# Feed-forward entry of a hybrid decoder block on one core: turned tiles and late sums kept in raw weight places, and the first product of the third weight pair moved ahead of the first pair's middle

## The chip, the cores and the metric

The kernel runs on one core of one Trainium2 chip. The metric is device time in microseconds (us) of one execution. Engines are named as the profile names them: PE (TensorE, matmuls), PEld (its weight loads), DVE (VectorE), ACT (ScalarE), POOL (GpSimd), SP (SyncE, which issues most DMAs; SPq is its queue). Each engine works through its own instructions in order and waits on semaphores for the others.

## The reference, cut to what matters

One decoder block over 1024 tokens of 1024 channels in float32: a state-space branch and a forgetting-attention branch, merged and projected, then cross-attention into 256 memory tokens, then the feed-forward part that the change is about, then a last normalisation.

```python
h = h + (gate_a * out_a + gate_b * out_b) @ w_mix_out[l]          # "mix"
h = h + memory_cross_attention(...)                               # ends with  o @ w_mem_o
f_a, f_b = jnp.split(rms_norm(h, norm_ffn[l]) @ w_ffn_in[l], 2, axis=-1)   # 1024 x (2 x 2816)
h = h + (jax.nn.silu(f_a) * f_b) @ w_ffn_out[l]                   # 2816 x 1024
return rms_norm(h, norm_final)
```

## The kernel before, in words

**Precision.** Every operand of a large product is split into a rounded high part and the remaining low part (`B.split`: ACT casts the high part, DVE subtracts for the low part), and each product is three matmuls: high x high, high x low, low x high (`mm3`, and `prod` in the feed-forward part). A matmul here has 512 columns.

**The feed-forward up-projection.** The hidden width 2816 is 22 blocks of 128. Block j needs 128 columns of the first half of `w_ffn_in` and 128 of the second: a "weight pair" of two 512 KB loads (`raw`, `rawb`). The product of a pair with the activations is done as seven half-size products in place of eight (Strassen's scheme in Winograd's form). Its left operands are sums of weight quarters, its right operands are quarters of the normalised and transposed ("turned") activations and sums of them: A11, A12, A22, S1, S2, S3, S4. Each product is 12 matmuls. Per pair the code has three parts:

- `start(j)`: products 1 (A11) and 2 (A12), into banks `mm` and `sc`; ACT and DVE then make silu of their sum.
- `middle(j)`: products 6 (S2), 7 (S3) and 5 (S1).
- `end(j)`: products 3 (S4) and 4 (A22), and the gated result.

The weights come from `w_first(j)` (products 1 and 2), `w_sums(j)` (5, 6, 7: `whi`/`wlo` and `we`) and `w_last(j)` (3, 4: `wdh`/`wdl`). From pair 2 on they are split on chip from `raw` and `rawb`. For pairs 0 and 1 (`AHEAD_IN = 2`) that was done much earlier, among the mix products (`ahead(j)`), and kept in DRAM (`w_d`), so that here they are only loaded.

**The entry.** `norm_blocks(t)` takes tile t of 128 tokens: DVE scales it (`xs`, line 220), PE turns it (line 226, eight 128x128 transposes into a `misc` and a `pv` bank), and the quarters and sums are split. Tiles 0 to 3 give A11 and A12; tiles 4 to 7 give the rest, and each needs the turned tile t - 4 again. In the kernel before, tiles 0 to 3 go to DRAM (`x_d`, 8 writes of 256 KB) and are read back as `xa` (4 reads of 512 KB). S4 and A22 are needed last, so their sources go to DRAM as well (`r_d`, 8 writes) and are read back in `norm_rest` as `xr` (4 reads).

**Order.** The code is recorded and then ordered by a scheduler that works from dependencies, so instructions of neighbouring steps are interleaved on each engine. Places in on-chip memory come from pools: "raw" has four places for weights before their split, "tmp" four places of 128 x 1024, "t" sixteen and "big" sixteen. A new tile waits until the last reader of the place is done. All the loads of the entry are issued by SP, in order.

Of the kernel before, what the change touches and what calls it, by code (L numbers as in the profile page):

```python
# [9 lines left out]
F32 = mybir.dt.float32  # L10
F32R = mybir.dt.float32r
# [8 lines left out]
P = 128  # L20
D = 1024
# [45 lines left out]
def f32(ap):  # L67
    return ap.bitcast(F32)
# [26 lines left out]
def weave(main, side, lead=0):  # L95

    n, m, done = len(main) - lead, len(side), 0
    for i, f in enumerate(main):
        f()
        want = m if i + 1 == len(main) else max(0, (i + 1 - lead) * m // max(n, 1))  # L100
        while done < want:
            side[done]()
            done += 1


class Shared:
# [3 lines left out]
        self.pool = pool  # L110

    def tmp(self, name, dt=F32):
        return self.pool.tile([P, D], dt, tag="tmp", bufs=4, name=name)

    def half(self, name, dt=F32):
        return self.pool.tile([P, 512], dt, tag="half", bufs=5, name=name)
# [386 lines left out]
def stage_tail(B, big, s2, sh, x, glu, aT, gate_d, kv_d, w_fox_o, w_mix_out, g_mq, w_mem_q, w_mem_o, g_ffn,  # L503
# [7 lines left out]
    def slot(dt=F32, name="t"):  # L511
        return s2.tile([P, D], dt, tag="t", bufs=NS2, name=name)
# [79 lines left out]


    AHEAD_IN = 2
    w_d = B.dram.tile([AHEAD_IN, 7, P, D], F32, name="w_d")
    pre = {}

    def ahead(j):

        def keep(n, t_):  # L600
            A.dma_start(w_d[j, n], f32(t_))

        def pair(n):
            hl = tmp("wph", F32R), tmp("wpl", F32R)
            return hl, [[t_[:, o:o + 512] for t_ in hl] for o in (0, 512)]

        def fetch():
            pre[j] = [tmp("wpr") for _ in range(2)]
            for r_, c in zip(pre[j], (0, FH)):
                S.dma_start(r_.rearrange("p (k c) -> p k c", k=8),  # L610
                            w_ffn_in[:, c + j * P:c + (j + 1) * P].rearrange("(k p) c -> p k c", p=P))

        def plain():
            hl, _ = pair(0)
            B.split(*hl, pre[j][0])
            for i, t_ in enumerate(hl):
                keep(i, t_)

        def sums():
            ra, rb = pre[j]  # L620
            b22 = rb[:, 512:]
            hl, (w5, w6) = pair(2)
            V.tensor_add(ra[:, 512:], ra[:, 512:], b22)
            V.tensor_add(ra[:, :512], ra[:, :512], rb[:, :512])
            V.tensor_add(rb[:, :512], rb[:, :512], b22)
            B.split(*w5, ra[:, :512])
            V.tensor_add(ra[:, 512:], ra[:, 512:], ra[:, :512])
            V.tensor_add(ra[:, :512], ra[:, :512], b22)
            B.split(*w6, ra[:, :512])
            for i, t_ in enumerate(hl):  # L630
                keep(2 + i, t_)

        def seventh():
            e_ = tmp("wph", F32R)
            B.split(e_[:, :512], e_[:, 512:], pre[j][1][:, :512])
            keep(4, e_)

        def rest():
            ra, rb = pre.pop(j)
            hl, (w3, w4) = pair(5)  # L640
            B.split(*w3, rb[:, 512:])
            B.split(*w4, ra[:, 512:])
            for i, t_ in enumerate(hl):
                keep(5 + i, t_)

        return [fetch, plain, sums, seventh, rest]

    wm0 = mix_weights(0)
    wm1 = mix_weights(1)
    mixes = [lambda t=t: mix(t, 0, wm0) for t in range(NT)] + [lambda t=t: mix(t, 1, wm1) for t in range(4)]  # L650
    weave(mixes, [f for j in range(AHEAD_IN) for f in ahead(j)], 4)
    for t in range(4, NT):
        mix(t, 1, wm1)
        norm(t - 4, gq, u2)
# [60 lines left out]
    def mem_out(t):  # L715
        oh, ol = oT[t // 4]
        for c in range(2):
            cs = slice(512 * c, 512 * c + 512)
            ps = B.bank()
            for h in range(MH):  # L720
                o = (h % 2) * 512 + (t % 4) * P
                B.mm3(ps, oh[h // 2][:, o:o + P], ol[h // 2][:, o:o + P], wo[h][0][:, 0, cs], wo[h][1][:, 0, cs],
                      h == 0, h == MH - 1)
            V.tensor_add(H[t][:, cs], H[t][:, cs], ps)
# [23 lines left out]

    NF = FH // P
    h_d = B.dram.tile([NT, P, D], F32, name="h_d")  # L750
    x_d = B.dram.tile([4, P, D], F32, name="x_d")
    r_d = B.dram.tile([4, P, D], F32, name="r_d")
    comb = {}

    def blocks(name, mk):
        if name not in comb:
# [3 lines left out]
    def put(name, mk, i, src, neg=False):  # L760

        hi_, lo_ = blocks(name, mk)
        for kk in range(2):
            sv = src[:, kk * 256:(kk + 1) * 256].rearrange("p (k c) -> p k c", k=2)
            hi, lo = [a[kk][:, :, i * P:(i + 1) * P] for a in (hi_, lo_)]
            if neg:
                A.activation(hi, sv, AF.Copy, scale=-1.0)
                V.scalar_tensor_tensor(out=lo, in0=sv, scalar=-1.0, in1=f32(hi), op0=ALU.mult, op1=ALU.subtract)
            else:
                B.split(hi, lo, sv)  # L770

    def norm_blocks(t):
        i = t % 4
        xs = s2.tile([P, D], F32, tag="xs", bufs=1, name="xs")
        B.norm_scale(xs, H[t], B.rstd(H[t]), gf)
        S.dma_start(h_d[t], H[t])
        ps = [B.turn(xs, b, ("misc", "pv")[b]) for b in range(2)]
        if t < 4:
            for b in range(2):
                xf = sh.half("xf")  # L780
                A.copy(xf, ps[b])
                S.dma_start(x_d[i][:, 512 * b:512 * b + 512], xf)
                put(("A11", "A12")[b], slot, i, xf)
            return
        xa, sx, s3 = tmp("xa"), tmp("sx"), sh.half("s3")
        S.dma_start(xa, x_d[i])
        a11, a12, s1n, a22 = xa[:, :512], xa[:, 512:], sx[:, :512], sx[:, 512:]
        A.copy(a22, ps[1])
        V.tensor_sub(s3, a11, ps[0])
        V.tensor_sub(s1n, ps[0], a22)  # L790
        V.tensor_sub(a11, s1n, a11)
        V.scalar_tensor_tensor(out=a12, in0=a11, scalar=-1.0, in1=a12, op0=ALU.mult, op1=ALU.subtract)
        put("S2", slot, i, a11)
        put("S3", bslot, i, s3)
        put("S1", bslot, i, s1n, neg=True)
        S.dma_start(r_d[i][:, :512], a12)
        S.dma_start(r_d[i][:, 512:], a22)

    def norm_rest(i):
        y = tmp("xr")  # L800
        S.dma_start(y, r_d[i])
        put("S4", bslot, i, y[:, :512])
        put("A22", bslot, i, y[:, 512:])

    raws, wts, ev = {}, {}, {}

    def w_fetch(j):
        raws[j] = B.wpool.tile([P, RAW], F32, tag="raw", bufs=4, name="raw")[:, :D], tmp("rawb")
        for r_, c in zip(raws[j], (0, FH)):
            f = S.dma_start(r_.rearrange("p (k c) -> p k c", k=8),  # L810
                            w_ffn_in[:, c + j * P:c + (j + 1) * P].rearrange("(k p) c -> p k c", p=P))
        return f

    def wpair(j):
        if j < 0:
            return slot(F32R, "wh0"), slot(F32R, "wl0")
        return [B.wpool.tile([P, WSLOT], F32R, tag=t_, name=t_)[:, :D] for t_ in ("whi", "wlo")]

    def w_kept(j, n, t_):
# [1 line left out]

    def w_first(j):

        if j < AHEAD_IN:
            a_ = wpair(j - 1 if j == 0 else j)
            for i, t_ in enumerate(a_):
                w_kept(j, i, t_)
            wts[j, 1], wts[j, 2] = [[t_[:, o:o + 512] for t_ in a_] for o in (0, 512)]
            return
        ra, rb = raws[j]  # L830
        a_ = wpair(j - 1 if j == 0 else j)
        B.split(*a_, ra)
        wts[j, 1], wts[j, 2] = [[t_[:, o:o + 512] for t_ in a_] for o in (0, 512)]

# [41 lines left out]
    def start(j):  # L876
        b1, b2 = ev[j, "b1"], _ = B.bank("mm"), B.bank("sc")
        prod(j, 1, b1, True)
        a0 = ev[j, "a0"] = sh.half("a0")
        A.copy(a0, b1)  # L880
        prod(j, 2, b2, True)
        V.tensor_add(a0, a0, b2)
        A.activation(a0, a0, AF.Silu)
# [63 lines left out]
    wo = [B.wblock(w_mem_o, k, 1, 0, D) for k in range(MH)]  # L947
    weave([lambda t=t: mem_out(t) for t in range(4)], cross(1) + [lambda t=t: norm_blocks(t) for t in range(2)])
    w_first(0)
    weave([lambda t=t: mem_out(t) for t in range(4, 8)], [lambda t=t: norm_blocks(t) for t in range(2, 6)])  # L950
    w_sums(0)
    start(0)
    norm_blocks(6)
    w_first(1)
    norm_blocks(7)
    start(1)
    w_fetch(2)
    w_last(0)
    w_sums(1)
    for i in range(4):  # L960
        norm_rest(i)
    middle(0)
    end(0)
    w_last(1)
    w_first(2)
    middle(1)
    w_sums(2)
    out_fetch(0, w_fetch(3).ins)
    for j in range(2, NF):
        start(j)  # L970
        end(j - 1)
        w_last(j)
        middle(j)
        if j + 1 < NF:
            w_first(j + 1)
            w_sums(j + 1)
        f = w_fetch(j + 2) if j + 2 < NF else f
        if j % 2:
            out_fetch(j // 2, f.ins)
        else:  # L980
            gated(j // 2 - 1)
# [859 lines left out]
```

## Time and profile before

| | |
|---|---|
| median of 3 runs | 1582.3 us (1581.09 to 1584.79) |
| profiled execution, its own time | 1584.62 us |
| its span, first to last instruction | 1582.9 us |
| mean granted TensorE clock | 0.985 |
| PE busy | 1536.4 us, 97% of the span, 7313 matmuls |
| DVE, ACT, POOL busy | 1026.6, 658.3, 266.8 us |

A PE that is busy 97% of the span is not yet a PE at its full pace: matmul ends are modelled, and a matmul at half clock is counted as busy for twice as long. So the stages are read by the starts of the matmuls and by the granted clock, not by the busy share. Names such as `mm<-S4h,wdh` stand for "output `mm` from inputs `S4h` and `wdh`"; text in brackets behind a row is the idle time of that engine before it and what ended it. The line numbers are those of the kernel before.

### The profile page before, as it was taken

Reading aid. Unit: us, or ns where it says so; the run is one execution under the profiler, and the core shown is the slowest. Engines: PE = TensorE matmul, PEld = TensorE weight load, DVE = VectorE, ACT = ScalarE, POOL = GpSimd, SP = SyncE. Lnnn points to the kernel's source line nnn. Section 1 sums busy time; section 2 is a strip of 40 time slices with the busy share of each in tenths; the row PEclk is TensorE's granted clock in tenths of the full one; section 3 lists DMA queues with packets and bytes.
Section 4 is the critical chain, followed back from the end, with each engine's and each line's share of the span. In section 5 each row is a group of like instructions: output and inputs, shape, how many; then the busy total and the mean of one; then the engine's idle time right before and its main releaser. Section 6 shows DMA issues by size and latency. Waiting matters only on the chain.

```text
span 1582.9 us, 20443 instructions
## 1 busy us (share of the span) xinstructions
PE 1536.4 (97%) x7313; PEld 1264.3 (80%) x7313; DVE 1026.6 (65%) x1822; ACT 658.3 (42%) x1177; POOL 266.8 (17%) x343
## 2 busy tenths in 40 slices
PE   7899999999999899999999999999999999999997
PEld 6688888898777678878888778888888888788886
DVE  6746545444788687685555687777777775566555
ACT  6422434422566553232335564333333333344342
POOL 3026653200212124110002200100000000001001
PEclk8899999999999899999999999999999999999999
DMA  8753466422123746367412186555544543897652
GB/s 294 151 105 100 131 118 138 111 103 30 26 45 59 203 121 199 109 206 248 138 45 76 54 282 236 172 165 162 159 160 156 162 147 129 269 392 228 192 160 107
DMA packets 197942, 240.87 MB, mean 152 GB/s; under 512 B 35448, under 2 KB 126488, under 8 KB 197328
## 3 DMA queue, kind: packets, MB, share of 16 engines
q1 hardware_dynamic: 190640, 222.79, 47.7%
q10 hardware_dynamic: 7200, 16.78, 2.8%
q8 instruction: 57, 0.93, 0.2%
q14 instruction: 45, 0.37, 0.1%
HBM read 165.60 MB, written 75.86 MB: 153 GB/s over the span
## 4 chain that ended last, share of the span: by engine, by line
PE 83%; DVE 6%; DMA 5%; ACT 3%; issue 1%; POOL 1%; SPq 0%; POOLq 0%; ACTq 0%; DVEq 0%
PE mm L873 15%; PE mm L168 8%; PE mm L170 8%; PE mm L169 8%; PE pv L873 7%; PE mm L1010 4%; PE sc L873 4%; PE sc L168 3%; PE sc L169 3%; PE sc L170 3%; PE sc L1010 3%; PE pv L1010 3%; PE misc L1010 1%; DMA raw<-in_w_in_dram 1%; PE mm L1623 1%
## 5 line engine op out<-in xcount | busy, mean ns | idle before, releaser
L178 ACT CAST whi<-raw 128x1024 fp32r<-128x1024 f32 (+2 forms) x124 | 115.8, 940 | 172.3 <-PE mm L873 44.0
L179 DVE TENSOR_TENSOR wlo<-raw,whi 128x1024 fp32r<-128x1024 f32 (+2 forms) x121 | 130.0, 1079 | 74.4 <-ACT whi L178 72.3
L168 PE MATMUL mm<-uh,whi 128*128 128x512 f32 x344 | 138.7, 403 | 2.4 <-ACT whi L178 2.3
L170 PE MATMUL mm<-uh,wlo 128*128 128x512 f32 x344 | 136.7, 398 | 0.5 <-DVE wlo L179 0.5
L179 DVE TENSOR_TENSOR ol<-or,oh 128x1024 fp32r<-128x1024 f32 x73 | 92.2, 1267 | 68.6 <-ACT oh L178 67.5
L169 PE MATMUL mm<-ul,whi 128*128 128x512 f32 x344 | 136.7, 397 | 0.0
L178 ACT CAST oh<-or 128x1024 fp32r<-128x1024 f32 x73 | 76.8, 1053 | 104.1 <-PE mm L1010 33.6
L905 POOL TENSOR_TENSOR g<-a,c 128x512 f32<-128x512 f32 x22 | 37.9, 1723 | 390.1 <-ACT a L904 371.0
L1660 POOL TENSOR_TENSOR pl<-pf,ph 128x512 fp32r<-128x512 f32 (+1 forms) x32 | 37.9, 1183 | 244.4 <-DVE ph L1659 174.5
L168 PEld LDWEIGHTS mm<-uh,whi 128*128 128x128 f32 x344 | 65.9, 192 | 14.9 <-ACT whi L178 2.7
L170 PEld LDWEIGHTS mm<-uh,wlo 128*128 128x128 f32 x344 | 65.8, 191 | 14.9 <-DVE wlo L179 1.5
L169 PEld LDWEIGHTS mm<-ul,whi 128*128 128x128 f32 x344 | 65.9, 192 | 11.2
L197 POOL TENSOR_TENSOR r<-ms,mhalf 128x1 f32<-128x1 f32 (+1 forms) x30 | 19.4, 649 | 307.3 <-DVE ms L193 279.9
L1657 ACT ACTIVATE pf<-sc 128x512 f32<-128x512 f32 (+1 forms) x96 | 46.4, 490 | 45.6 <-DVE sc L1653 29.9
L873 PE MATMUL pv<-S3h,we 128*128 128x512 f32 x176 | 58.1, 389 | 0.0
L1663 DVE TENSOR_TENSOR pl<-pf,ph 128x512 fp32r<-128x512 f32 (+2 forms) x64 | 36.2, 567 | 9.8 <-ACT ph L1662 9.0
L1126 POOL TENSOR_TENSOR sg<-sg,ga 128x512 f32<-128x512 f32 x16 | 29.7, 1881 | 73.5 <-DVE sg L1119 60.1
L1010 PE MATMUL mm<-ol,oh 128*128 128x512 f32 x106 | 41.2, 389 | 0.0
L1010 PE MATMUL mm<-oh,ol 128*128 128x512 f32 x106 | 41.2, 389 | 0.0
L1010 PE MATMUL mm<-oh 128*128 128x512 f32 x106 | 41.2, 389 | 0.0
L168 PE MATMUL sc<-uh,whi 128*128 128x512 f32 x104 | 40.8, 392 | 0.0
L168 PE MATMUL mm<-yh,whi 128*128 128x512 f32 x104 | 40.7, 392 | 0.0
(583 smaller groups left out, 4563.7 us busy)
## 6 DMA issues: line engine op xcount, KB each, us to landing
or<-c_d SPq DMA_DIRECT2D x77, 256.0 KB
raw<-in_w_in_dram SPq DMA_DIRECT2D x22, 512.0 KB
wo<-in_w_ffn_out_dram SPq DMA_DIRECT2D x22, 512.0 KB
c_d<-g SPq DMA_DIRECT2D x44, 256.0 KB
t_d<-wo SPq DMA_DIRECT2D x44, 256.0 KB
or<-t_d SPq DMA_DIRECT2D x44, 256.0 KB
raw<-in_w_ffn_in_dram SPq DMA_DIRECT2D x20, 512.0 KB
rawb<-in_w_ffn_in_dram SPq DMA_DIRECT2D x20, 512.0 KB
```

Source lines behind the costliest of these rows:

```text
L168: T.matmul(ps, lh, rh, start=first, stop=False)
L169: T.matmul(ps, lh, rl, start=False, stop=False)
L170: T.matmul(ps, ll, rh, start=False, stop=last)
L178: self.A.copy(hi, src)
L179: (self.G if pool_lo else self.V).tensor_sub(lo, src, f32(hi))
L873: T.matmul(ps, l_[:, k, :], r_, start=first and k == 0 and i == 0, stop=k == 3 and i == 2, skip_group_check=True)
L905: G.tensor_mul(g[:, 512:], a1, c1)
L1010: T.matmul(ps, l_[:, gi], r_[:, 512:], start=n < 3 and p == 0 and k == 0 or n == 7 and p == 0 and k == 0, stop=p == NP - 1 and k == 2, ski ...
L1126: self.B.G.tensor_mul(self.out[j][:, cs], self.out[j][:, cs], ga)
L1657: self.exp = A.activation(pf[:, off:], ps[:, off:], AF.Exp)
L1660: G.tensor_sub(pl[:, off:], pf[:, off:], f32(ph[:, off:]))
L1663: V.tensor_sub(pl[:, off:], pf[:, off:], f32(ph[:, off:]))
```

## The change

The four raw weight places, which in the kernel before receive the first parts of the pairs 2 to 5 while cross-attention runs, now hold the four turned tiles 0 to 3 (`kept[i]`, tile name `xf`). `x_d` and `r_d` are gone. Tile t reads `kept[t - 4]` in place, overwrites it with the sources of S2 and S4, keeps A22's source in its `tmp` tile `sx`, and `norm_rest` splits from these two. `tmp` gets a fifth place. `norm_rest` is held behind the splits of S1 of tile 7 (`B.behind`).

The high and low part of pair 2's first weights are now made among the mix products too (`first` and the existing `plain`, one more load of 512 KB and two more writes to `w_d`), and are loaded in the entry. `start(2)` then comes before `middle(0)`, right behind tile 7, where before only `start(0)` and `start(1)` did.

```diff
     def tmp(self, name, dt=F32):
-        return self.pool.tile([P, D], dt, tag="tmp", bufs=4, name=name)
+        return self.pool.tile([P, D], dt, tag="tmp", bufs=5, name=name)
...
-    w_d = B.dram.tile([AHEAD_IN, 7, P, D], F32, name="w_d")
+    w_d = B.dram.tile([AHEAD_IN + 1, 7, P, D], F32, name="w_d")
...
-        return [fetch, plain, sums, seventh, rest]
+        def first():
+            pre[j] = [tmp("wpr")]
+            S.dma_start(pre[j][0].rearrange("p (k c) -> p k c", k=8),
+                        w_ffn_in[:, j * P:(j + 1) * P].rearrange("(k p) c -> p k c", p=P))
+
+        return [fetch, plain, sums, seventh, rest] if j < AHEAD_IN else [first, plain]
...
-    weave(mixes, [f for j in range(AHEAD_IN) for f in ahead(j)], 4)
+    weave(mixes, [f for j in range(AHEAD_IN + 1) for f in ahead(j)], 4)
...
     def norm_blocks(t):
...
         if t < 4:
+            kept[i] = B.wpool.tile([P, RAW], F32, tag="raw", bufs=4, name="xf")[:, :D]
             for b in range(2):
-                xf = sh.half("xf")
+                xf = kept[i][:, 512 * b:512 * b + 512]
                 A.copy(xf, ps[b])
-                S.dma_start(x_d[i][:, 512 * b:512 * b + 512], xf)
                 put(("A11", "A12")[b], slot, i, xf)
             return
-        xa, sx, s3 = tmp("xa"), tmp("sx"), sh.half("s3")
-        S.dma_start(xa, x_d[i])
+        xa, sx, s3 = kept[i], tmp("sx"), sh.half("s3")
...
-        put("S1", bslot, i, s1n, neg=True)
-        S.dma_start(r_d[i][:, :512], a12)
-        S.dma_start(r_d[i][:, 512:], a22)
+        last = put("S1", bslot, i, s1n, neg=True)
+        kept[i] = a12, a22
+        return last
 
     def norm_rest(i):
-        y = tmp("xr")
-        S.dma_start(y, r_d[i])
-        put("S4", bslot, i, y[:, :512])
-        put("A22", bslot, i, y[:, 512:])
+        a12, a22 = kept.pop(i)
+        put("S4", bslot, i, a12)
+        put("A22", bslot, i, a22)
...
     def w_first(j):
-        if j < AHEAD_IN:
-            a_ = wpair(j - 1 if j == 0 else j)
+        if j <= AHEAD_IN:
+            a_ = wpair(j - 2)
...
     w_first(0)
+    w_first(1)
     weave([lambda t=t: mem_out(t) for t in range(4, 8)], [lambda t=t: norm_blocks(t) for t in range(2, 6)])
-    w_sums(0)
     start(0)
     norm_blocks(6)
-    w_first(1)
-    norm_blocks(7)
+    w_first(2)
     start(1)
-    w_fetch(2)
+    last = norm_blocks(7)
+    w_sums(0)
+    start(2)
     w_last(0)
     w_sums(1)
-    for i in range(4):
-        norm_rest(i)
+    with B.behind(last[0]), B.behind(last[1]):
+        for i in range(4):
+            norm_rest(i)
+    w_fetch(2)
     middle(0)
     end(0)
     w_last(1)
-    w_first(2)
     middle(1)
     w_sums(2)
     out_fetch(0, w_fetch(3).ins)
     for j in range(2, NF):
-        start(j)
+        if j > AHEAD_IN:
+            start(j)
         end(j - 1)
```

What the scheduler makes of it is seen in the order of the instructions. On PE, before, the end of `start(0)` (bank `sc`, A12), then the turns of tiles 6 and 7 (`misc` and `pv` from `xs`) with the first products of `start(1)` (`whi`, `wlo`) between them:

```order
L873 MATMUL sc<-A12h,wl_8559 128x512
L226 MATMUL misc<-ident,xs 128x128 x4
L226 MATMUL pv<-ident,xs 128x128 x4
L873 MATMUL mm<-A11h,whi 128x512
L873 MATMUL mm<-A11l,whi 128x512
L873 MATMUL sc<-A12h,whi 128x512
L226 MATMUL pv<-ident,xs 128x128 x4
L226 MATMUL misc<-ident,xs 128x128 x4
L873 MATMUL mm<-A11h,wlo 128x512
```

The same two turns in the changed kernel, first tile 6 inside `start(1)` (its weights are now called `wh` and `wl` too), then tile 7 between `start(1)` and `start(2)` (`whi`, `wlo`):

```order
L875 MATMUL mm<-A11h,wh 128x512
L226 MATMUL misc<-ident,xs 128x128 x4
L226 MATMUL pv<-ident,xs 128x128 x4
L875 MATMUL mm<-A11l,wh 128x512
L875 MATMUL mm<-A11h,wl 128x512
L875 MATMUL sc<-A12h,wh 128x512
```

```order
L875 MATMUL sc<-A12h,wl 128x512
L226 MATMUL misc<-ident,xs 128x128 x4
L226 MATMUL pv<-ident,xs 128x128 x4
L875 MATMUL mm<-A11h,whi 128x512
L875 MATMUL mm<-A11l,whi 128x512
```

Ten products of `start(1)` now stand between `start(0)` and the turn of tile 6, the other fourteen between the two turns, and all 24 of `start(2)` behind the second. The products of S2, S3 and S1 follow those.

On SP, before, the DMA issues from the second last store of the residual tiles (`h_d`) to the weights of pair 1's sums:

```order
L776 DMA h_d<-h_6744 128x1024
L797 DMA r_d<-sx 128x512
L786 DMA xa<-x_d 128x1024
L820 DMA whi<-w_d 128x1024
L796 DMA r_d<-xa 128x512
L820 DMA wlo<-w_d 128x1024
L797 DMA r_d<-sx 128x512
L820 DMA we<-w_d 128x1024
L796 DMA r_d<-xa 128x512
L786 DMA xa<-x_d 128x1024
L820 DMA whi<-w_d 128x1024
L820 DMA wlo<-w_d 128x1024
```

In the changed kernel, from the end of the same kept weights on (`rawb` and `raw` are the loads of pair 2 and following from `w_ffn_in`):

```order
L822 DMA wdl<-w_d 128x1024
L822 DMA we<-w_d 128x1024
L812 DMA rawb<-in_w_ffn_in_dram 128x8x128
L812 DMA raw<-in_w_ffn_in_dram 128x8x128 x2
L822 DMA wdh<-w_d 128x1024
L812 DMA raw<-in_w_ffn_in_dram 128x8x128 x2
L812 DMA rawb<-in_w_ffn_in_dram 128x8x128
L940 DMA wo_9221<-in_w_ffn_out_dram 128x1024
L822 DMA wdl<-w_d 128x1024
```

No `x_d`, `xa`, `r_d` or `xr` stands between the loads of the kept weights any more. The four `raw` loads, which stood ahead of the first `h_d`, now stand here; the first of them waits for a low part of S4 of tile 0 (its place in "raw"), the next three for those of tiles 1, 2 and 3.

On DVE the splits of S4 and A22 stood, before, behind the weight sums of pair 2 (`raw` and `rawb`):

```order
L851 TENSOR_TENSOR raw<-raw 128x512
L179 TENSOR_TENSOR wlo<-raw,whi 128x512
L179 TENSOR_TENSOR wlo<-raw,whi 128x1024
L895 SCALAR_TENSOR_TENSOR c_9121<-c_9121,pv 128x512
L852 TENSOR_TENSOR raw<-raw,rawb 128x512
L179 TENSOR_TENSOR S4l<-xr,S4h 128x2x128
L179 TENSOR_TENSOR wlo<-raw,whi 128x512
```

In the changed kernel they come first, right behind tile 7's S1 and the sum in `start(2)` (line 884):

```order
L771 SCALAR_TENSOR_TENSOR S1l<-sx,S1h 128x2x128 x2
L884 TENSOR_TENSOR a_9016<-a_9016,sc 128x512
L179 TENSOR_TENSOR S4l<-xf,S4h 128x2x128 x4
L179 TENSOR_TENSOR A22l<-sx,A22h 128x2x128
L179 TENSOR_TENSOR S4l<-xf,S4h 128x2x128
L179 TENSOR_TENSOR A22l<-sx,A22h 128x2x128 x3
```

The weight sums of pair 2 follow behind all sixteen splits, and the split of pair 2's first weights is no longer here.

More of the change, by code (lines that the diff above doesn't have):

```diff
@@ L750, in stage_tail @@
     h_d = B.dram.tile([NT, P, D], F32, name="h_d")
-    x_d = B.dram.tile([4, P, D], F32, name="x_d")
-    r_d = B.dram.tile([4, P, D], F32, name="r_d")
-    comb = {}
+    comb, kept = {}, {}
     def blocks(name, mk):
@@ L766, in put @@
             if neg:
-                A.activation(hi, sv, AF.Copy, scale=-1.0)
-                V.scalar_tensor_tensor(out=lo, in0=sv, scalar=-1.0, in1=f32(hi), op0=ALU.mult, op1=ALU.subtract)
+                last = A.activation(hi, sv, AF.Copy, scale=-1.0), \
+                    V.scalar_tensor_tensor(out=lo, in0=sv, scalar=-1.0, in1=f32(hi), op0=ALU.mult, op1=ALU.subtract)
             else:
                 B.split(hi, lo, sv)
+        return last if neg else None
     def norm_blocks(t):
@@ L815, in wpair @@
         if j < 0:
-            return slot(F32R, "wh0"), slot(F32R, "wl0")
+            return slot(F32R, "wh"), slot(F32R, "wl")
         return [B.wpool.tile([P, WSLOT], F32R, tag=t_, name=t_)[:, :D] for t_ in ("whi", "wlo")]
@@ L830, in w_first @@
         ra, rb = raws[j]
-        a_ = wpair(j - 1 if j == 0 else j)
+        a_ = wpair(j)
         B.split(*a_, ra)
```

## The prediction

> **What bounds the kernel now.** I read the page first, then the chain of waits, then the stretch of the feed-forward entry: the stage windows, PE's timeline there, and DVE's and SP's beside it.
>
> ```profile
> span 1582.9 us, 20443 instructions
> PE 1536.4 (97%) x7313; PEld 1264.3 (80%) x7313; DVE 1026.6 (65%) x1822; ACT 658.3 (42%) x1177; POOL 266.8 (17%) x343
> PE 83%; DVE 6%; DMA 5%; ACT 3%; issue 1%; POOL 1%; SPq 0%; POOLq 0%; ACTq 0%; DVEq 0%
> ```
>
> PE sets the time, so a change off PE is worth only what PE stops waiting. In the chain, once the feed-forward loop runs, PE is followed by PE alone:
>
> ```profile
> 1008.46 2.72 PE pv L873 x12
> 1011.18 5.44 PE mm L873 x24
> ```
>
> One product of 12 matmuls costs 2.72 us, 0.227 us a matmul. At that pace nothing can be gained but by taking PE's holes away. The entry has one. The windows (PE busy, PEld, DVE, ACT, POOL, then the granted clock, DMA share, GB/s):
>
> ```profile
> 938.00:940.00 2.00, 2.00 (x10) 1.51 (x9) 2.00 (x9) 1.98 (x3) 0.00 (x0) 1.00 0.97 326
> 940.00:942.00 2.00, 0.25 (x2) 0.00 (x0) 1.58 (x6) 0.48 (x2) 0.55 (x1) 1.00 0.95 347
> 942.00:944.00 2.00, 1.13 (x6) 1.16 (x7) 0.96 (x3) 0.20 (x1) 0.00 (x0) 0.62 0.92 359
> 944.00:946.00 2.00, 1.02 (x5) 0.62 (x4) 1.53 (x2) 1.15 (x3) 0.00 (x0) 0.50 0.58 231
> 946.00:948.00 2.00, 2.00 (x7) 1.60 (x8) 2.00 (x5) 0.84 (x4) 0.00 (x0) 0.50 0.94 352
> 948.00:950.00 2.00, 2.00 (x10) 1.83 (x9) 2.00 (x6) 1.12 (x3) 0.00 (x0) 0.68 0.93 291
> ```
>
> PE stands idle from 940, and then the granted clock is halved until after 948, which the busy share hides. PE's timeline through it (start, duration, in brackets the idle time before):
>
> ```profile
> 933.76 0.60 PE L226 MATMUL misc<-ident,xs 128*128 128x128 f32 x4
> 934.55 0.48 PE L873 MATMUL mm<-A11h,wh 128*128 128x512 f32 x1
> ...
> 939.86 0.39 PE L873 MATMUL sc<-A12h,wl 128*128 128x512 f32 x1
> 942.87 1.08 PE L226 MATMUL misc<-ident,xs 128*128 128x128 f32 x4 [2.63 <-DVE rt L205]
> ...
> 945.79 0.79 PE L873 MATMUL mm<-A11h,whi 128*128 128x512 f32 x1 [0.98 <-DMA whi<-w_d]
> 946.38 0.63 PE L873 MATMUL mm<-A11l,whi 128*128 128x512 f32 x1
> ...
> 948.80 0.71 PE L873 MATMUL mm<-A11h,wlo 128*128 128x512 f32 x1
> 949.34 0.40 PE L873 MATMUL mm<-A11h,whi 128*128 128x512 f32 x1
> ```
>
> `start(0)` leaves PE free at 939.86 + 0.23 = 940.09. It then waits for the scaled tile 6, then for the weights of pair 1, whose load took long among the `x_d` and `r_d` traffic. The chain gives that load by itself: issued at 939.08, landed 6.67 us later.
>
> ```profile
> 939.08 6.67 DMA whi<-w_d
> ```
>
> **The change part by part.** *The hole.* From 940.09 to 949.34 are 9.25 us. The work issued in it is two turned tiles (at full clock one takes 934.55 - 933.76 = 0.79 us, so 1.58) and four matmuls (0.91). So 9.25 - 2.49 = 6.76 us are lost, by idling and by the half clock together. That is the most that this place can give.
>
> *What fills it.* The weights of `start(1)` now take free places of the pool "t" and are loaded behind the fourth `h_d`, which leaves SP at 904.56:
>
> ```profile
> 877.74 26.82 SPq L776 DMA_DIRECT2D h_d<-h  x4
> ```
>
> That is some 35 us ahead, so PE goes on from `start(0)` into `start(1)`. It reaches the turn of tile 6 after ten of its products, at 940.09 + 2.27 = 942.36. The tile comes from DVE:
>
> ```profile
> 941.45 1.28 DVE L220 SCALAR_TENSOR_TENSOR xs<-h,r,gbc 128x1024 f32<-128x1024 f32 x1
> 944.47 0.69 DVE L789 TENSOR_TENSOR s<-xa,misc 128x512 f32<-128x512 f32 x1 [1.48 <-DMA xa<-x_d]
> 945.08 1.28 DVE L220 SCALAR_TENSOR_TENSOR xs<-h,r,gbc 128x1024 f32<-128x1024 f32 x1
> 946.28 0.68 DVE L790 TENSOR_TENSOR sx<-misc,sx 128x512 f32<-128x512 f32 x1
> 948.75 0.76 DVE L179 TENSOR_TENSOR S2l<-xa,S2h 128x256 fp32r<-128x256 f32 x2
> 949.42 0.75 DVE L768 SCALAR_TENSOR_TENSOR S1l<-sx,S1h 128x256 fp32r<-128x256 f32 x2
> ```
>
> DVE's order up to this `xs` is unchanged, so the turn still starts near 942.87: a wait of 0.5 us stays. Tile 7's `xs` no longer waits for `xa`: `s` can start behind the turn of tile 6, at about 943.6 in place of 944.47, and `xs` ends near 945.4. PE gets to that turn at 942.87 + 0.79 + 14 x 0.227 = 946.84, without a wait. `start(2)` follows, 0.79 + 5.44 us, to 953.07.
>
> The first product of `middle(0)` needs S2 of tile 7. For tile 6 DVE needed 949.42 - 945.08 = 4.34 us from the start of `xs` to the end of the S2 splits. Tile 7 has no second `xs` in between (-1.2) and follows tile 6's S1 (0.67) and the sum of `start(1)` (0.6). I put tile 6's S1 end at 949.15, the sum at 949.75, and from there `s` (0.61), the way from `sx` to the first S2 split (948.75 - 946.28 = 2.47) and that split (0.42): 953.25. PE wants it one matmul after 953.07, at 953.30. The two are level, and I allow 0.2 us of wait. So 0.7 us of the hole stay: 6.76 - 0.7 = **6.1 us gained**.
>
> *The kept weights of the entry.* Those for `start(2)` and pair 0's sums take the places of `w_mem_o`, free when the turn at 933.76 starts; 6.67 us later, 940.4, is ahead of 947.6. `we`, `wdh` of pair 0 wait for the end of `start(0)`, its `wdl` and pair 1's `we` for that of `start(1)`, 946.84; with 6.67 us they land at 946.8 and 953.5, before S3 (956) and S4 want them. Cost nothing.
>
> *S4 and A22.* `x_d` and `r_d` were 24 DMAs of 8 MB in all, the last of them behind weights for which PE must first be done with a place:
>
> ```profile
> 968.15 0.32 SPq L820 DMA_DIRECT2D wdl<-w_d  x1
> 968.99 0.32 SPq L801 DMA_DIRECT2D xr<-r_d  x1
> 973.33 0.71 ACT L178 CAST S4h<-xr 128x256 fp32r<-128x256 f32 x2 [3.05 <-DMA xr<-r_d]
> 974.30 0.39 PE L873 MATMUL mm<-S4h,wdh 128*128 128x512 f32 x1
> ```
>
> Before, PE came to S4 at 974.30 with no idle time, since the scheduler had put pair 1's middle and 18 matmuls of `start(2)` in front. Now S4 follows S2, S3, S1 and nine matmuls of pair 1's S2: 953.3 + 8.16 + 2.04 = 963.5. DVE has tile 7's S1 done at 954.4, `start(2)`'s sum at 955.0 and all sixteen splits, each 0.335 apart, at 960.4, so 3 us early. ACT's casts for them run one split ahead. I cost it at nothing; if each split took its 0.42 us alone, it would be ready at 961.7, still early.
>
> *The raw loads.* They are the price of the raw places:
>
> ```profile
> 839.01 25.50 SPq L810 DMA_DIRECT2D raw<-in_w_ffn_in_dram  x4
> ```
>
> Before, they lay 90 us ahead. Now the first may be issued when two S4 splits are done, about 955.7, the next at 956.4. With the 6.67 us of the slowest load above they land by 963.1. DVE is free of its splits at 960.4, and needs for pair 2's sums and pair 3's first split 4 x 0.6 + 0.6 + 1.14 + 0.6 + 0.6 = 5.3 us, with one result of pair 0 between them that waits for S4's end at 966.2. So S2's weights of pair 2 are there at 968.4. PE wants them after S4, A22, the rest of pair 1's S2, S3 and S1: 963.5 + 5.44 + 0.68 + 5.44 = 975.1. Cover 6.7 us, cost nothing; beyond that each us late is a us lost. Behind these loads on SP stand pair 1's `wdh`, two more `raw`, `rawb` of pair 3, `wo` and pair 1's `wdl`; the first of them to be wanted is `wdh`, at S4 of pair 1, behind 975.
>
> ```profile
> 959.33 0.69 DVE L845 TENSOR_TENSOR raw<-raw,rawb 128x512 f32<-128x512 f32 x1
> 963.57 1.23 DVE L179 TENSOR_TENSOR wlo<-raw,whi 128x1024 fp32r<-128x1024 f32 x1 [1.01 <-ACT whi L178]
> ```
>
> *The third pair among the mix products* adds one load, two writes, one cast and one subtraction, and puts one `wpr` load ahead of the sixth block of `w_mix_out`, in a stretch where the DMA engines are full:
>
> ```profile
> 700.00:710.00 10.00, 9.63 (x42) 7.63 (x42) 8.56 (x12) 4.82 (x6) 0.00 (x0) 1.00 1.00 321
> 710.00:720.00 10.00, 10.00 (x45) 8.12 (x44) 9.41 (x15) 4.54 (x8) 0.00 (x0) 1.00 0.99 308
> 720.00:730.00 10.00, 10.00 (x46) 8.28 (x45) 3.92 (x6) 1.19 (x2) 0.00 (x0) 1.00 0.57 203
> ```
>
> The bounds: nothing, if PE's mix products stay covered as they do at 720 (46 matmuls in 10 us is the full pace), and 5.1 us, if all 1.57 MB at 308 GB/s came onto PE's path. The moved load alone is 0.52 MB, 1.7 us. The three others come late, when the DMA share is down to 0.57, so I take 0 and keep 1.7 in the range. The fifth `tmp` place can only loosen waits here; a gain has the PE idle of these windows as its bound, below 1 us.
>
> **The sum.** The profiled execution took 1584.6 us, 2.3 above the median. 1584.6 - 6.1 = 1578.5 for it, and 1582.3 - 6.1 = **1576.2 us** for the median.
>
> **The rivals.** *The clock drops all the same* (chance 0.12). The 0.5 us at tile 6 may be longer, if DVE's chain is late, and halve the clock. For it: a hole of 2.63 us was enough before. Against it: an idle time of 1.11 us in the stretch before left the clock at 1.00.
>
> ```profile
> 886.28 0.63 PE L698 MATMUL misc<-ident,pe 128*128 128x128 f32 x4 [1.11 <-DVE ptl L179]
> 880.00:890.00 10.00, 8.32 (x46) 6.34 (x44) 7.66 (x20) 5.84 (x21) 3.67 (x5) 1.00 0.14 54
> ```
>
> The half clock lasted from within 942 to 944 until within 948 to 950, some 6.8 us, so it would cost half of that on a PE that has work: 3.4 us, time 1579.6. [...]
>
> *The mix stretch pays* (0.10): the moved load puts 1.7 us or more on PE, time 1578 to 1581. It shows as idle time or fewer than 44 matmuls per 10 us between 700 and 760.
>
> *Pair 2's weights come late, slower than before* (0.04). SP issues in order, and the raw loads stand behind ten loads of kept weights, each of which waits for a place and for an older DMA. If raw and `rawb` land after 975.1 - 5.3 = 969.8, PE waits at S2 of pair 2. It decides against the change from 969.8 + 6.1 = 975.9 on; at 980 the time is 1586.4. Against it: 24 DMAs fewer compete, and issue at 956 would have to take 20 us.
>
> *The hole is filled, but PE waits again right behind it* (0.08): S2 or S3 of tile 7 or the weights of pair 0's sums are late by the same 3 us that the r_d reads were; a gain of about 3, time 1579.3. DVE is the engine to look at, since it is busy through the whole stretch.
>
> **How the numbers follow.** Forecast 0.66: gain 5 to 7.5, 1574.8 to 1577.3, the upper gain with 0.7 us of other waits. A measurement tells about 0.2%, 3.2 us, from no change: faster means below 1579.1. Faster is the forecast and, of the others, about half of the 0.30 that end near 1579 to 1580: 0.82. Same 0.14, slower 0.04. The range reaches from 1573.0, the whole hole plus the noise of the median (1581.09 against 1582.3) and 1.3 of earlier waits, to 1580.2, the clock rival with some noise.
>
> **What would show it.** PE's starts through `start(0)`, `start(1)`, `start(2)` 0.227 apart, with one wait below 1 us before the turn of tile 6; the granted clock at 1.00 in all windows of the entry; no row that waits for `raw` before S2 of pair 2; 44 or more matmuls per 10 us at 700 to 760. Wrong it is if the clock still falls to 0.50 there, if PE waits more than 2 us between 942 and 976, or if the gain of the entry is lost before 760 or behind 1351, where nothing was changed.

## The result, and the profile after

The changed kernel takes 1580.34 us (median of 22 runs, 1576.02 to 1583.63) against 1584.68 us of the kernel before in the same comparison (22 runs, 1581.09 to 1590.83; the three runs shown ahead of the prediction are among these, and their median was 2.4 us lower). The ratio is 0.9971, 95% interval 0.9963 to 0.9980: 4.6 us less, 3.2 to 5.9, so faster by 0.2 to 0.4%. Predicted were 6.1 us. The profiled execution took 1578.99 us.

The page of the changed kernel, its span and busy times:

```profile
span 1577.3 us, 20371 instructions
PE 1529.5 (97%) x7313; PEld 1258.4 (80%) x7313; DVE 1023.0 (65%) x1822; ACT 657.7 (42%) x1177; POOL 264.9 (17%) x343
```

PE still has 7313 matmuls and is still busy for 97%: as before, the share shows nothing. The windows over the old hole do (PE busy, PEld, DVE, ACT, POOL, granted clock, DMA share, GB/s):

```profile
942.00:944.00 2.00, 1.91 (x13) 1.75 (x14) 1.41 (x4) 0.80 (x3) 0.00 (x0) 1.00 0.95 363
944.00:946.00 2.00, 2.00 (x10) 1.63 (x9) 2.00 (x4) 1.61 (x5) 0.00 (x0) 1.00 0.55 221
946.00:948.00 2.00, 2.00 (x14) 1.77 (x13) 2.00 (x6) 1.30 (x4) 0.00 (x0) 1.00 0.32 84
```

The clock is at 1.00 where it was 0.62, 0.50 and 0.50, and each window has 10 to 14 matmuls (the short transposes of the turns included) where it had 5 to 7. PE's timeline (start, duration, in brackets the idle time before it) has two waits left between `start(0)` and pair 3:

```profile
933.84 0.47 PE L875 MATMUL mm<-A11h,wh 128*128 128x512 f32 x1
...
941.45 0.39 PE L875 MATMUL mm<-A11h,wh 128*128 128x512 f32 x1
942.09 0.63 PE L226 MATMUL misc<-ident,xs 128*128 128x128 f32 x4 [0.26 <-DVE rt L205]
...
946.23 0.60 PE L226 MATMUL misc<-ident,xs 128*128 128x128 f32 x4
...
974.26 0.39 PE L875 MATMUL mm<-S1h,wlo 128*128 128x512 f32 x1
...
975.85 0.39 PE L875 MATMUL mm<-S2h,whi 128*128 128x512 f32 x1
976.96 0.50 PE L875 MATMUL mm<-S4h,wdh 128*128 128x512 f32 x1 [0.72 <-ACT c L896]
...
1013.58 0.39 PE L875 MATMUL mm<-S4h,wdh 128*128 128x512 f32 x1
```

By the starts (0.227 us belong to the matmul ahead) the turn of tile 6 costs 942.09 - 941.45 - 0.227 = 0.41 us, and S4 of pair 1 costs 976.96 - 975.85 - 0.227 = 0.88 us.

**A measure that is finer than the run's time.** Single runs of one kernel differ by 6 to 10 us, and the profiles show that most of it arises long before the feed-forward part (last section). So each profile is also measured from the first matmul of `start(0)` to the first of S4 of pair 3, the first and last row above. The same 352 matmul instructions lie between in every version, 336 of 512 columns and 16 transposes (the filled hole has its 38 fill matmuls besides). At full pace they take 336 x 0.2267 (2.72 us for 12) + 1.58 for two turned tiles = 77.75 us. The kernel before took 1019.18 - 934.55 (the row at 934.55 stands in the prediction):

```profile
1019.18 0.39 PE L873 MATMUL mm<-S4h,wdh 128*128 128x512 f32 x1
```

| kernel | first matmul of start(0) | S4 of pair 3 | stretch | gain in it | ratio of the times to before (95%) |
|---|---|---|---|---|---|
| before | 934.55 | 1019.18 | 84.63 | | |
| changed | 933.84 | 1013.58 | 79.74 | 4.89 | 0.9971 (0.9963 to 0.9980) |
| kept places only | 933.57 | 1017.27 | 83.70 | 0.93 | 0.9994 (0.9979 to 1.0008) |
| third pair only | 932.95 | 1017.13 | 84.18 | 0.45 | 1.0003 (0.9991 to 1.0015) |
| before, hole filled | 930.56 | 1014.24 | 83.68 | 0.95 | 1.0002 (0.9990 to 1.0014) |
| copy first | 938.70 | 1017.47 | 78.77 | 5.86 | 0.9963 (0.9950 to 0.9976) |
| turn later too | 936.93 | 1015.32 | 78.39 | 6.24 | 0.9964 (0.9951 to 0.9977) |
| four tmp places | 933.57 | 1014.81 | 81.24 | 3.39 | 0.9978 (0.9965 to 0.9992) |
| late raw loads | 932.12 | 1012.51 | 80.39 | 4.24 | 0.9971 (0.9959 to 0.9983) |

The 5.6 us between the two spans are 4.89 in this stretch and 0.71 ahead of `start(0)`; what lies behind pair 3 adds up to nothing. The 0.71 cannot be credited to the change, since `start(0)` begins anywhere from 930.56 to 938.70 in these profiles.

There is one profile of each kernel. The wait at the turn of tile 6, which the changed kernel and five of the versions share, comes out at 0.41 to 0.51 us in all six, which is a hint of how far a stretch can be trusted. By the times of the runs, none of the last four versions can be told from the changed kernel; what is said of them rests on the stretch.

### The profile page after: what moved, and what is told of

The parts are those of the page before. It is cut to its first block, busy times and chain, and to the rows that moved or that the text cites. A ratio compares the mean times of both kernels' runs of the same rounds, so it can differ in the third digit from the quotient of the medians.

```text
span 1577.3 us, 20371 instructions
## 1 busy us (share of the span) xinstructions
PE 1529.5 (97%) x7313; PEld 1258.4 (80%) x7313; DVE 1023.0 (65%) x1822; ACT 657.7 (42%) x1177; POOL 264.9 (17%) x343
## 4 chain that ended last, share of the span: by engine, by line
PE 80%; DVE 7%; DMA 5%; ACT 3%; POOL 2%; issue 2%; SPq 0%; POOLq 0%; ACTq 0%; DVEq 0%
PE mm L875 14%; PE mm L168 8%; PE mm L169 8%; PE mm L170 8%; PE pv L875 7%; PE mm L1015 4%; PE sc L875 4%; PE sc L168 3%; PE sc L170 3%; PE sc L169 3%; PE sc L1015 3%; PE pv L1015 3%; PE misc L1015 1%; DMA raw<-in_w_in_dram 1%; DMA raw<-in_w_mem_kv_dram 1%
## 5 line engine op out<-in xcount | busy, mean ns | idle before, releaser
L178 ACT CAST we<-rawb 128x512 fp32r<-128x512 f32 x20 | 12.5, 624 | 68.9 <-PE pv L875 33.8
```

The source lines that it names most:

```text
L178: self.A.copy(hi, src)
```

## The experiments

**Kept places only: what is the gain made of?** The third pair is taken back: `start(2)` stands in the loop again and its weights are split on chip.

```diff
-        if j <= AHEAD_IN:
+        if j < AHEAD_IN:
...
     norm_blocks(6)
-    w_first(2)
     start(1)
     last = norm_blocks(7)
     w_sums(0)
-    start(2)
...
+    w_first(2)
     middle(1)
...
-        if j > AHEAD_IN:
-            start(j)
+        start(j)
```

> The changed kernel without the third pair: the turned tiles and late sums stay in the raw places, start(1) is still loaded early, but start(2) stands in the loop again, behind middle(0), and its weights are split on chip. Theory (the gain is PE work that covers DVE's chain of tiles 6 and 7): behind start(1), at about 947, PE has nothing but S2 and S3 of tile 7, whose splits the changed kernel has ready at about 952.5; so PE idles some 5 us there, in one piece, the clock falls to 0.50 behind it, and of the gain of the entry (4.9 us) nothing or at most 1.5 us is left: ratio to the kernel before 0.999 to 1.002. Rival (the gain is the 24 DMAs of turned tiles that are gone): PE waits less than 2 us there and the ratio stays at 0.997 to 0.998.

```profile
949.91 0.50 PE L875 MATMUL pv<-S3h,we 128*128 128x512 f32 x1 [2.91 <-ACT S3h L178]
```

PE's timeline has one long wait, behind `start(1)` and the turn of tile 7, for S3 of that tile; and the windows show that the clock falls behind it, for ((1 - 0.72) + (1 - 0.50) + (1 - 0.92)) x 2 / 0.5 = 3.4 us:

```profile
950.00:952.00 2.00, 2.00 (x6) 1.34 (x7) 2.00 (x6) 2.00 (x8) 0.00 (x0) 0.72 0.88 260
952.00:954.00 2.00, 2.00 (x6) 1.55 (x5) 2.00 (x7) 2.00 (x8) 0.00 (x0) 0.50 0.00 0
954.00:956.00 2.00, 2.00 (x9) 1.64 (x8) 2.00 (x7) 2.00 (x8) 0.00 (x0) 0.92 0.18 49
```

The wait is 3.1 us by the starts and not 5, since S3 can start before S2. The matmuls at half clock behind it, from 949.91 to 954.39, take 1.8 us more than at full pace, about half of the 3.4. Together that is 4.9; the 0.88 us at S4 of pair 1 are not lost here, since `start(2)` stands ahead of it again, so 4.0 are lost on balance, and 0.93 of the 4.89 us are left. The theory holds: with the tiles on chip, but without products that are ready, the hole only moves by one `start`.

**Third pair only.** The counterpart: order, weights and `tmp` of the changed kernel, but the turned tiles and late sums in DRAM again.

```diff
-            kept[i] = B.wpool.tile([P, RAW], F32, tag="raw", bufs=4, name="xf")[:, :D]
...
+                xf = sh.half("xf")
                 A.copy(xf, ps[b])
+                S.dma_start(x_d[i][:, 512 * b:512 * b + 512], xf)
...
-        xa, sx, s3 = kept[i], tmp("sx"), sh.half("s3")
+        xa, sx, s3 = tmp("xa"), tmp("sx"), sh.half("s3")
+        S.dma_start(xa, x_d[i])
...
+        y = tmp("xr")
+        S.dma_start(y, r_d[i])
```

> The changed kernel with the turned tiles and late sums in DRAM again (x_d, r_d, xa, xr as before), everything else as changed: third pair ahead, start(1) and start(2) loaded early, five tmp places. Theory: the hole from 940 to 949 is filled by start(1) and start(2) just the same, the clock stays at 1.00, and the ratio is 0.996 to 0.998; waits of up to 2 us where xa or xr are late. Rival (kept tiles are what the gain needs): xa comes so late among the kept weights that PE idles over 4 us behind start(2) or at S4, and the ratio is 0.999 or above.

The rival came true, in three waits of about 4 us together and not in one. The three longest of PE's waits from 930 to 1000, grouped (us in total, times, longest):

```profile
PE mm L880 <- ACT S4h L178: 1.4, 1, 1.4
PE mm L880 <- ACT c L901: 1.4, 1, 1.4
PE mm L880 <- ACT S2h L178: 1.0, 1, 1.0
```

```profile
949.99 0.69 DVE L795 TENSOR_TENSOR s<-xa,misc 128x512 f32<-128x512 f32 x1 [1.76 <-DMA xa<-x_d]
```

```profile
964.19 0.71 ACT L178 CAST S4h<-xr 128x256 fp32r<-128x256 f32 x2 [1.75 <-DMA xr<-r_d]
```

The hole at 940 is gone and the clock stays at 1.00, but S2, S4 and a copy `c` behind them are late. S2 of tile 7 is late because DVE's first step for that tile, `s`, waits for `xa` until 949.99. For S4, SP issued the first `xr` at 955.46, behind ten loads of kept weights, and ACT could begin with the sixteen casts only at 964.19, where the changed kernel has the last of them behind it. That is 31.2 us behind the first matmul of `start(0)`, as in the kernel before (965.97, 31.4 us): S4's sources come no later than they did, but PE now wants them some 6 us sooner. Of 4.89 us 0.45 are left. So neither half of the change is worth 1 us alone, and the two together 4.89: the third pair gives PE work for the time that DVE needs for tile 7, and the kept places take the sources of S2 and S4 off the way through DRAM, on which they come too late for that order. Both versions keep the early weights of `start(1)` and the fifth `tmp` place; what the early weights are worth alone was not tried.

**The hole of the kernel before, filled: clock or data?**

```diff
     start(0)
+    one = B.ident.bitcast(BF16)
+    fill = B.bank("sc")
+    for _ in range(21):
+        T.matmul(fill[:, :2 * P], one[:, :P], one, start=True, stop=True)
     norm_blocks(6)
+    for _ in range(17):
+        T.matmul(fill[:, :2 * P], one[:, :P], one, start=True, stop=True)
```

> The kernel before, with idle time of the hole filled by matmuls that nothing reads: 21 behind start(0), 17 more behind the turn of tile 6 (256 columns, 0.21 us each at half clock in the first 4 us of the profile, so about 0.11 at full). Nothing else changes but that the scheduler puts the turn of tile 7 ahead of the four matmuls of start(1). Theory (the clock falls because PE idles; the hole itself is waiting for data): the granted clock stays at 1.00 from 940 to 950, but the turn of tile 7 still waits for its xs (946.4) and the products for whi and wlo, so the hole shrinks by 1 to 2 us only; ratio 0.998 to 1.000. Rival (the half clock is what costs, 3.4 us): 3 us or more are gained, ratio 0.998 or below. Third way (the clock falls whatever PE does): the fill runs at 0.2 us a matmul, ends behind 945, and the kernel is 1 to 3 us slower.

```profile
936.10 2.46 PE L956 MATMUL sc<-ident 128*128 128x256 bf16 x21
938.88 0.63 PE L226 MATMUL misc<-ident,xs 128*128 128x128 f32 x4 [0.32 <-DVE rt L205]
...
939.78 2.02 PE L959 MATMUL sc<-ident 128*128 128x256 bf16 x17
...
942.46 0.63 PE L226 MATMUL misc<-ident,xs 128*128 128x128 f32 x4 [0.19 <-DVE sx L790]
...
943.07 0.48 PE L873 MATMUL mm<-A11h,whi 128*128 128x512 f32 x1
```

The clock is 1.00 in every window of this entry, as the theory and the rival said, and the fill runs at 0.11 us a matmul. The 0.21 us of the first 4 us, put down to half clock in the expectation, stand in windows with a granted clock of 1.00 (before, 2 to 6), so that cause was the author's estimate. From the end of `start(0)` (936.10) to the first product of `start(1)` (943.07) are 6.97 us with two turns (1.58) in them, so 5.39 us are still lost, against 6.76. The stretch gains 0.95 us, just under the 1 to 2 us of the theory (0.4 of the 1.37 go into small steps behind the hole), and the time does not change measurably. Most of the hole was therefore waiting for the turns, that is for `xs`; the weights were there by 943.07, when `start(1)` went on without a wait. The half clock lay mostly over time that PE had to wait anyway. What the change had to bring was ready work, not a warm clock.

**The copy first: the 0.88 us at S4 of pair 1.** Products 5 (S1) and 3 (S4) of a pair go into the same `mm` bank, and between them ACT must copy it (`c`). In the loop `start(j + 1)` stands between the two; for pair 1 `start(2)` has been moved away, and seven matmuls of pair 2's S2 are all that is left. ACT, in its order:

```profile
974.85 1.57 ACT L178 CAST whi<-raw 128x512 fp32r<-128x512 f32 x2 [0.99 <-DVE raw L854]
976.32 0.58 ACT L896 COPY c<-mm 128x512 f32<-128x512 f32 x1
```

S1 is done at 974.26 + 0.23, but two casts of pair 3's weights (one of its sums, one of its first weights) stand ahead of the copy, and the first of them waits for DVE. The edit holds them behind the copy:

```diff
...
-            w_first(j + 1)
-            w_sums(j + 1)
+            with B.behind(cc if j == 2 else None):   # cc: the copy c of pair 1
+                w_first(j + 1)
+                w_sums(j + 1)
```

> The changed kernel with one step of order: the sums of pair 3 are held behind ACT's copy c of pair 1, so that the copy is not queued behind the two casts of pair 3. Theory (the 0.88 us that PE loses ahead of S4 of pair 1 come from ACT's order): the copy runs about 974.8 in place of 976.3, PE's row at S4 of pair 1 has no wait, and all later products are 0.7 to 0.9 us earlier than in the changed kernel; span 1576.4 to 1576.8. Rival (PE is short of ready work there, whoever does the copy): the wait stays or moves to the weights of pair 3, which come later now, and the span stays within 0.3 us of the changed kernel's 1577.3.

```profile
979.95 0.39 PE L875 MATMUL mm<-S2h,whi 128*128 128x512 f32 x1
980.18 0.49 PE L875 MATMUL mm<-S4h,wdh 128*128 128x512 f32 x1
```

The wait is gone with only four matmuls of S2 in between, and the stretch is 0.97 us shorter (78.77 against 79.74), a little more than the 0.7 to 0.9 expected. The expected span was missed, 1581.2 against 1576.4 to 1576.8: this execution reached `start(0)` at 938.70, 4.9 us later than that of the changed kernel, for reasons ahead of the entry. The cause is settled by the stretch; a span was the wrong thing to forecast.

**The turn later too.** The turn of tile 6 is put between the two products of `start(1)` (which takes a function to call there), behind twelve matmuls in place of ten. (Where the text ahead of the result counts ten, fourteen and 24 "products" of a `start`, these are matmuls; a product has twelve of them.)

```diff
...
-    norm_blocks(6)
+    start(1, lambda: norm_blocks(6))
     w_first(2)
-    start(1)
```

> The kernel of the copy-first experiment, and the turn of tile 6 put behind all twelve matmuls of the first product of start(1), in place of behind ten. Theory (the 0.41 us at tile 6 are PE being two matmuls early for xs): PE has no wait row from start(0) to S4 of pair 3, and this stretch, 84.63 us in the kernel before, 79.74 in the changed one and 78.77 with the copy first, takes 78.3 to 78.5. Rival: tile 7's chain on DVE follows the later turn, S2 of tile 7 is late by what the turn gained, and the stretch stays at 78.6 to 78.9.

```profile
944.96 0.39 PE L875 MATMUL mm<-A11h,wl 128*128 128x512 f32 x1
945.21 0.63 PE L226 MATMUL misc<-ident,xs 128*128 128x128 f32 x4
```

No wait row is left on PE from 925 to 1000, and the stretch takes 78.39 us, as the theory had it. Of the remaining 0.64 us over the full pace, 0.45 are five steps of about 0.09 us, at the first matmul behind each turned tile and of S4; the rest is spread thinly. By the run's time this kernel (1579.61 us, 11 runs) is faster than the kernel before, but cannot be told from the changed one; in the stretch it is 1.35 us shorter.

**Four tmp places.**

```diff
-        return self.pool.tile([P, D], dt, tag="tmp", bufs=5, name=name)
+        return self.pool.tile([P, D], dt, tag="tmp", bufs=4, name=name)
```

> The changed kernel with four tmp places in place of five. Theory (the fifth place is worth less than 1 us anywhere): the stretch from start(0) to S4 of pair 3 takes 79.7 +- 0.4 us and the time is that of the changed kernel. Rival (the fifth place carries part of the gain, since rawb of the pairs 2 and 3 and the sx of four tiles all want one): rawb of pair 3 comes later, the sums of pair 2 or 3 with it, and the stretch takes 81 us or more.

The rival again: 81.24 us, 1.50 more; the load that comes late first is pair 2's `rawb`, where the rival named pair 3's. SP issues it at 956.20, where the changed kernel does at 947.08, ahead of the raw loads. DVE's sums of pair 2 start 1.6 us later and those of pair 3 behind them, and on ACT the copies `c` stand behind their casts: that of pair 0 behind a cast for pair 2 (shown), that of pair 1 behind the two casts for pair 3.

```profile
956.20 0.38 SPq L812 DMA_DIRECT2D rawb<-in_w_ffn_in_dram  x1
```

```profile
960.96 0.69 DVE L847 TENSOR_TENSOR raw<-raw,rawb 128x512 f32<-128x512 f32 x1 [1.76 <-DMA rawb<-in_w_ffn_in_dram]
```

```profile
962.28 0.62 ACT L178 CAST whi<-raw 128x512 fp32r<-128x512 f32 x1 [3.94 <-DVE raw L848]
962.81 0.58 ACT L896 COPY c<-mm 128x512 f32<-128x512 f32 x1
```

```profile
963.44 0.50 PE L875 MATMUL mm<-S4h,wdh 128*128 128x512 f32 x1 [0.77 <-ACT c L896]
...
978.18 0.50 PE L875 MATMUL mm<-S4h,wdh 128*128 128x512 f32 x1 [1.28 <-ACT c L896]
```

Without the fifth place 1.50 of the 4.89 us are lost, and it acts through ACT's order at S4 of the pairs 0 and 1: by the starts PE loses 0.93 us at the first and 1.44 at the second, where the changed kernel loses 0 and 0.88.

**Late raw loads.** Pair 2's loads are held behind the last kept weights of pair 1 on SP.

```diff
...
-    w_fetch(2)
     middle(0)
     end(0)
-    w_last(1)
+    with B.tc.issue_after(w_last(1)):   # its last load
+        w_fetch(2)
```

> The changed kernel with the raw loads of pair 2 held behind the last kept weights of pair 1, so that they are issued about 968.5 in place of 955 and land about 971.5. Theory (the prediction's threshold: late from a landing at 969.8 on, each us later a us lost): the sums come at about 976.8, and the stretch from start(0) to S4 of pair 3 is 1 to 3 us longer than the changed kernel's 79.74. Rival (S4 and A22 of pair 1 can go first, so that S2 of pair 2 is wanted only at about 980): PE waits nowhere for raw, and the stretch stays within 0.5 us or gets shorter, since ACT's copy c of pair 1 has no cast of pair 3 ahead of it.

Two PE waits behind 970, then DVE's first sum of pair 2, and ACT's copy:

```profile
972.53 0.39 PE L875 MATMUL mm<-S1h,wlo 128*128 128x512 f32 x1
973.64 0.50 PE L875 MATMUL mm<-S4h,wdh 128*128 128x512 f32 x1 [0.73 <-ACT c L896]
...
979.01 0.39 PE L875 MATMUL pv<-A22h,wdl 128*128 128x512 f32 x1
979.65 0.50 PE L875 MATMUL mm<-S2h,whi 128*128 128x512 f32 x1 [0.25 <-ACT whi L178]
```

```profile
973.93 0.69 DVE L847 TENSOR_TENSOR raw<-raw,rawb 128x512 f32<-128x512 f32 x1 [6.41 <-DMA rawb<-in_w_ffn_in_dram]
```

```profile
973.01 0.58 ACT L896 COPY c<-mm 128x512 f32<-128x512 f32 x1 [4.38 <-PE mm L875]
```

The sums could start only at 973.93, and PE lost 0.41 us to them (979.65 - 979.01 - 0.23); the stretch is 0.65 us longer than the changed kernel's. That is not the theory's 1 to 3 us, and nearer to the rival's 0.5: the order on PE was made for late weights, S4 and A22 of pair 1 went first, and S2 of pair 2 was wanted only at 979.2. The 0.88 us at S4 of pair 1 are there again (973.64 - 972.53 - 0.23), now with an idle ACT: without any matmul between S1 and S4, the copy itself (0.58 us) and the way to and from it cost as much as the queue on ACT did.

## Why the prediction was right, and where it was not

**The time and the base.** 1576.2 us was predicted, 1580.34 measured, 0.14 us above the upper end of the range of 1573.0 to 1580.2. 2.4 us of the difference are the base (1582.3 of three runs, 1584.68 of 22), the other 1.8 a gain of 4.3 between the medians (4.6 by the ratio) in place of 6.1. On the base that the prediction had, the ratio gives 1582.3 x 0.9971 = 1577.7, inside the range and below the 1579.1 from which it called the kernel faster. The gain is below the forecast's 5 to 7.5, though the interval of 3.2 to 5.9 reaches into it.

**The hole** was the right place and the right size. All of its 6.76 us came back except the 0.41 at tile 6 (predicted 0.5). The turn of tile 7 was reached without a wait (946.23; predicted 946.84 for a `start(0)` that began 0.71 us later). The 0.2 us at S2 of tile 7 were not needed.

**The step that failed** is in the paragraph on the raw loads: "PE wants them after S4, A22, the rest of pair 1's S2, S3 and S1", and from there on only the weights were asked for. What product 3 of pair 1 itself waits for, the copy `c`, was not priced, though the change takes away just the matmuls that cover it in the loop. It cost 0.88 us. 6.76 - 0.41 - 0.88 = 5.47; the stretch gained 4.89, and the 0.6 between are the steps of up to 0.1 us that also stand in the version without any wait. It is the fourth rival in small ("PE waits again right behind it"), at a place that it did not name; DVE, which it pointed to, holds up ACT's casts there, and ACT the copy. That S4 of pair 0 cost nothing, as said, was partly luck: its copy `c` was not priced either, and in the changed kernel it ended at 962.73, 0.06 us ahead of S4 at 962.79.

```profile
962.15 0.58 ACT L896 COPY c<-mm 128x512 f32<-128x512 f32 x1
```

**The raw loads** cost nothing, as said. The last split for pair 2's S2 on DVE in the changed kernel:

```profile
966.45 0.68 DVE L179 TENSOR_TENSOR wlo<-raw,whi 128x512 fp32r<-128x512 f32 x1
```

It ended at 967.1, and PE took its first matmul of that product at 974.49: 7.4 us of cover, predicted 6.7. The threshold was wrong, though: the late loads landed 4.1 us behind the 969.8 that was to decide, and cost 0.41. It had PE's order as fixed, but the order itself follows the loads.

**The fifth tmp place** was mis-sized and misplaced: "below 1 us", and looked for among the mix products. It is worth 1.50 us in the entry.

**The mix stretch** cost 0, the value taken. From a product just ahead of it to a `misc` turn behind it, before and changed:

```profile
704.21 0.50 PE L168 MATMUL pv<-ath,whi 128*128 128x512 f32 x1 [0.37 <-DVE gb L536]
...
899.83 0.66 PE L698 MATMUL misc<-ident,pe 128*128 128x128 f32 x4 [0.19 <-POOL pe L689]
```

```profile
703.27 0.50 PE L168 MATMUL pv<-ath,whi 128*128 128x512 f32 x1 [1.24 <-DVE gb L536]
...
899.13 0.66 PE L703 MATMUL misc<-ident,pe 128*128 128x128 f32 x4 [0.20 <-POOL pe L694]
```

195.62 us before and 195.86 changed; the 1.7 us kept for it in the range were not needed. The sign "44 or more matmuls per 10 us at 700 to 760" was met from 710 on (45 or 46) but not at 700 to 710, where the changed kernel has 38 and the kernel before 42. That is the wait of 1.24 us for `gb` ahead of the mix stretch; in the other five versions with the third pair it is 0.42 to 0.58 us, so it does not come with the change.

**The clock rival** did not come: the wait at tile 6, 0.26 us of idle time, left the clock at 1.00. Its price, half of 6.8 us on a PE that has work, was not put to the test: the filled hole, where 3.4 us did not come back but 0.95, had a PE that waited. With the kept places only, where PE has work behind its wait, the clock fell for 3.4 us, half of what the rival took, and cost 1.8.

## What to carry to other kernels

A hole in front of a bound engine is filled by work that is ready, so look for what makes other work ready (here one early weight pair and four tiles less on the queue, neither of which gains 1 us alone); keeping the clock up with empty work gave back only the part that was not waiting, here 1.37 of 6.76 us. When a block of matmuls is moved to fill a hole, ask what it covered where it stood: here it hid a copy out of a bank between two products. And where single runs scatter by more than the effect, measure the stretch between two fixed instructions in the profiles.

## What the runs showed of the hardware that was not expected

**The half clock comes in pieces of about 3.4 us.** Among the small products near 374, in the kernel before (it ends in the window from 378):

```profile
374.00:376.00 2.00, 1.92 (x7) 1.30 (x8) 1.71 (x7) 0.00 (x0) 0.00 (x0) 0.96 0.03 7
376.00:378.00 2.00, 2.00 (x6) 1.53 (x6) 0.88 (x3) 0.00 (x0) 0.00 (x0) 0.50 0.00 0
378.00:380.00 2.00, 2.00 (x8) 1.61 (x7) 0.85 (x2) 0.00 (x0) 0.00 (x0) 0.68 0.00 0
```

(0.04 + 0.50 + 0.32) x 2 / 0.5 = 3.4 us at half clock. In the entry of the kernel before it was (0.38 + 0.50 + 0.50 + 0.32) x 4 = 6.8 us, twice that, and with the kept places only 3.4 again. In the changed kernel's profile, where the program is the same at this place, the clock was 1.00 from 374 to 380.

**The length of the idle time alone does not decide.** The same turn near 72, first before, then with the third pair only, each with its window:

```profile
71.39 0.63 PE L226 MATMUL misc<-ident,xt 128*128 128x128 f32 x4 [1.90 <-DVE ul L179]
...
72.00:74.00 2.00, 2.00 (x8) 1.56 (x7) 1.90 (x3) 0.37 (x1) 1.52 (x1) 0.52 0.46 161
```

```profile
72.67 0.63 PE L226 MATMUL misc<-ident,xt 128*128 128x128 f32 x4 [2.56 <-DVE ul L179]
...
72.00:74.00 2.00, 1.33 (x8) 1.21 (x9) 1.91 (x2) 0.43 (x2) 2.00 (x1) 1.00 0.55 192
```

Behind 1.90 us of idle time the clock fell, behind 2.56 us it did not. It also fell behind 2.63 us (the entry of the kernel before) and 2.91 us (kept places only). Near 374 the same two idle times, 0.81 and 0.62 us (to 0.01 us), stand in the PE rows of five profiles: the clock fell behind them in three (before, third pair only, copy first) and stayed at 1.00 in two (changed, kept places only). What does decide was not shown: no run here moved an idle time and left the rest as it was.

Each piece costs about half its length where PE has work: from the matmul behind the 0.62 us to the 24th after it, the starts lie 7.4 us apart in two profiles with a piece of 3.4 us there (before, third pair only) and 5.8 in three without (changed, kept places only, hole filled). Which executions get one near 72 (six of nine) or 374 (four of nine), and how long it is near 520 (3.4, 6.8 or 10.2 us), differs. That is a part of why `start(0)` began anywhere from 930.56 to 938.70 in the nine profiles. The latest, copy first at 938.70, has 37.5 us at half clock ahead of it and the changed kernel, at 933.84, has 23.9, which at half the length is 6.8 us where 4.9 lie between them (an estimate); but the kernel before has 34.1 and began at 934.55, so it is not the whole. Filling those gaps as the entry's was filled was not tried.
